# A two-layer attention and state-space kernel on one core: a new order for its opening

## The chip, the cores and the metric

The kernel runs on one core of one Trainium2 chip. A core has a tensor engine (PE; PEld is its weight load), a vector engine (DVE), a scalar engine (ACT), GpSimd (POOL) and a sync engine (SP) that here issues nearly all DMAs. Every engine works through its own instruction list in order and waits on semaphores. The metric is device time in microseconds (us): 1477.1 us, the median of three runs (1476.56 to 1478.08).

## The reference

Two layers work on one sequence of 512 tokens with 1024 features, in float32. What matters here is the way into the first layer:

```
h = rms_norm(x, norm_g[i])
(c_q, c_kv, k_rope, gate_a, z, xbc, ...) = split(h @ w_in[i])
o_a = mla(c_q, c_kv, k_rope, cos, sin) * silu(gate_a)     # rotated by cos, sin of the positions
o_b = ssd(z, xbc, dt_raw)                                 # state-space branch
o_c = sparse_attention(..., rel_bias[bucket(pos_q - pos_k)]) * silu(gate_c)
x = x + (g_a*(o_a @ w_br_a) + g_b*(o_b @ w_br_b) + g_c*(o_c @ w_br_c)) @ w_out[i]
x = x + sigmoid(x @ w_ple_gate[i]) * (p[i] @ w_ple[i])
```

Three things in it do not need `h`: `p @ w_ple`, the bias table `rel_bias[bucket(...)]`, and the cosines and sines of the positions. They can be worked out before the first layer's tiles.

## The kernel before

Activations lie as [feature, token]: a tile is 128 features by 512 tokens. A float32 product is made of three: activations and weights are each split into a high and a low part (ACT copies the high part, DVE subtracts it to get the low part), and `mm` multiplies high by high (L235), low weights by high (L236) and high by low (L243). `wload` issues one weight load of 512 KB on SP (L223), the copy on ACT (L224) and the subtraction on DVE (L225).

The order of PE is that of the Python code (`manual_schedule` for PE). DVE, ACT, POOL and SP get their lists from a scheduler by priority, so the place of an instruction there is not that of its line. All lists are fixed when the program is built.

The opening of layer 0 works like this:

- `setup` loads two tiles of p and their first weights. `rel_setup` loads positions and the bias's 32 rows with SP (L326 to L334), and makes thresholds and steps of the bias on POOL and DVE (L335 to L359).
- `run` loads the eight tiles of x on SP (L1313); `stat_add` squares each on ACT (L405) and adds it up on DVE (L406).
- `ple` makes p @ w_ple, four tiles of six products for each of two weight units. PE has these products to fill its time.
- `rel_bias` makes the distance bias in 32 blocks; a block is four mask tiles (DVE L376, some on ACT L374), 12 narrow products on PE (L388), an eviction (L392) and a store. The numbers in `EARLY` say how many blocks PE gets at four places of the opening: six in all. PRE, POST and PLE0 say how many pieces of `ple` come before, among and behind the sums of x's norm.
- `stat_sum` sums the squares on PE (L415), and a chain of 12 small DVE instructions (L424 to L430) makes 1 / rms. `stat_rows` spreads it over the partitions (PE L437). `normed` makes h: DVE multiplies (L448), ACT copies the high part (L449), DVE subtracts (L453), eight tiles.
- `rope_tables` makes the cosine and sine tables: one small load, 17 small DVE instructions, two sines on ACT with a table load, four stores to DRAM, two loads back, behind `normed`.
- `prep` starts the layer: the helper `three` multiplies three tiles of weights with all of h (L682, L683, L686: 72 products). Then come the c_q tiles, a second norm (L415 to L437 again), and the rotation of the keys (`rope`, L641 to L644), which needs the tables.

PSUM tiles of tag "mm" have three buffers; the high and low weights have three buffers each and the raw ones two.

Of the kernel before, what the change touches and what calls it, by code (L numbers as in the profile page):

```python
"""Two layers of MLA + SSD + sparse attention with a gated merge, activations kept [feature, token]."""
# [36 lines left out]
# smallest distance that falls into each of the 32 distance buckets  # L38
# [3 lines left out]
# ---------------------------------------------------------------- columns of w_in, in the order used here  # L42
# [13 lines left out]
# units of weights: 128 partitions of up to 1024 numbers  # L56
# [13 lines left out]
for _i in range(4):  # L70
    # followed by the keys of the two heads, from w_ukv
    _unit(("uq", _i), "uq", [96 * _h + _d for _h in (2 * _i, 2 * _i + 1) for _d in range(64)])
# [15 lines left out]
# ---------------------------------------------------------------- layout of the per-feature vectors  # L88
# [8 lines left out]
def pack(i):  # L97
    """Inputs laid out for the kernel; nothing is computed."""
    o = {}
# [41 lines left out]
    # numbers that depend on shapes alone  # L141
# [11 lines left out]
    for k in range(5):  # L153
        c[:, 408 + k] = 4.0 * (r >= 128 - 32 * k)  # the last k groups of 32 rows
# [4 lines left out]
class Build:  # L159
# [19 lines left out]
    # ---- SBUF in slots of 2 KB per partition  # L179
# [28 lines left out]
    # ---- weights: load, split into two parts of 12 bits each whose sum is exact  # L208
# [19 lines left out]
    def mm(self, ps, w, off, acts, t=slice(0, T)):  # L228
        """ps[128 features, tokens] += W^T act over the k tiles of acts, float32 from parts"""
# [23 lines left out]
    # ---- constants and tables  # L253
    def setup(self):
# [7 lines left out]
        self.prefetch(0, ("ple", 0))  # L262
        self.rel_setup()
# [18 lines left out]
    def rope_tables(self):  # L282
        """cosines, and sines with their signs, 32 rows four times over; worked out as [16 frequencies x 8, 64 tokens]"""
# [16 lines left out]
        # the rounding of k may leave r a little outside of [-pi, pi]  # L300
# [17 lines left out]
    def rel_setup(self):  # L318
        """positions from the first one on, thresholds, and the steps of the distance bias from bucket to bucket"""
        nc, I, cc = self.nc, self.I, self.c  # L320
        nc.sync.dma_start(cc[:, 384:416], I["c"][:, 384:416])
        # one row per bucket and query of four
# [3 lines left out]
        nc.sync.dma_start(d[:, 0], bass.AP(tensor=rb.tensor, offset=rb.offset, ap=[[8, 32], [0, 4], [1, 8]]))  # L326
        nc.sync.dma_start(d[4:128, 1], bass.AP(tensor=rb.tensor, offset=rb.offset, ap=[[8, 31], [0, 4], [1, 8]]))
        self.posi = self.slot(I32)
        nc.sync.dma_start(self.posi, bass.AP(tensor=I["pos"].tensor, offset=I["pos"].offset, ap=[[0, 128], [1, T]]))
        p0 = self.posi[:, 0:1]  # L330
        pq = self.slot(I32, (128, 128))
        nc.sync.dma_start(pq, I["posq"])
        last = self.const.tile([128, 1], F32, name="rbl")
        nc.sync.dma_start(last, bass.AP(tensor=rb.tensor, offset=rb.offset + 8 * 31, ap=[[0, 16], [1, 8], [1, 1]]))  # L334
# [4 lines left out]
        # masks of 0 and 1 take the steps, masks of -1 and 1 take half of them, and half of their sum is added  # L339
# [21 lines left out]
    def rel_bias(self):  # L361
        """8 * rel_bias[bucket(pos_q - pos_k)] into DRAM as [head, query, key], by sums over the buckets'
        thresholds: 32 buckets of 4 queries are the 128 rows of a product."""
# [35 lines left out]
    # ---- root mean square over the features, for each token, on every partition (PSUM)  # L399
# [9 lines left out]
    def stat_sum(self, s, dim, cs=range(4), fill=None):  # L409
        """1 / rms, [token, block of 128 tokens]"""  # L410
# [29 lines left out]
    def normed(self, xs, g, R):  # L440
        """parts of x * g * R"""
# [19 lines left out]
    # ---- pieces of work are generators, which yield what they put on the tensor engine in units of 512 columns  # L461
# [13 lines left out]
    @staticmethod  # L475
    def mix(*gens):
        """in turns"""
        gens = list(gens)
        while gens:
            for g in list(gens):  # L480
                try:
                    yield next(g)
                except StopIteration:
                    gens.remove(g)

    def weave(self, main, n, *tracks):
        """n pieces of main with other work, lists of (generator, cost), each spread evenly over them"""
# [14 lines left out]
    # ---- one tile of h @ w_in  # L502
# [9 lines left out]
    def gate2(self, ps):  # L512
        """2 silu"""
# [6 lines left out]
    # ---- p @ w_ple / 2 into DRAM  # L520
# [24 lines left out]
    # ---- softmax of one block of 128 queries; its transpose goes to PT  # L545
# [11 lines left out]
    def turned(self, u, qt, PT):  # L557
        """parts of the transpose of one block of 128 queries, [keys, queries]"""
# [21 lines left out]
    def attention(self, logits, V, PT, done):  # L580
        """logits(h, qt): probabilities of one block of queries; V(h, kb): [128 keys, high | low].
        Three stages, each a block of queries behind the one before; two pieces per block."""
# [31 lines left out]
    def gated(self, o, g):  # L614
        """parts of o * (g / 2)"""
# [6 lines left out]
    # ---- tiles that several branches need  # L622
    def common(self, ps):
# [7 lines left out]
        # four sets of keys, two heads of which are in use; the rotated part is common to all heads  # L631
# [5 lines left out]
    def rope(self, t, hi, lo, r=slice(0, 128)):  # L637
        """parts of the rotated rows"""
# [9 lines left out]
    def mla_rope(self, l, i):  # L648
        """the rotated part of four heads' queries"""
# [19 lines left out]
    # ---- MLA  # L669
    def prep(self, l, more):  # L670
        """what the attention needs, the chains of one norm under the products of the next tiles"""
        nc = self.nc

        def three(names):
            """tiles side by side, as the parts of h arrive"""
# [67 lines left out]
    def mla_pair(self, l, j):  # L743
        """keys and queries of heads 2j and 2j + 1"""
# [53 lines left out]
    # ---- sparse attention  # L798
    def stacked(self, l, name, j, out):
        """two heads of 64: [high; low] of the first, [low; high] of the second"""  # L800
# [9 lines left out]
    def dsa_keys(self, l, ps):  # L810
# [9 lines left out]
        # values: [high | low] for each block of keys  # L820
# [5 lines left out]
    def index(self, l, j):  # L826
        """scores of two index heads, for the queries from 128 on"""
# [25 lines left out]
    def topk(self):  # L853
        """the 128 largest of each row, the first of equals first"""
# [45 lines left out]
    # ---- SSD  # L900
    def ssd_steps(self, l):
        """dt, its sums within the chunks, and the decays, [token, chunk and head]"""
# [15 lines left out]
        # log(1 + e) = 2 atanh(e / (2 + e))  # L918
# [38 lines left out]
    def conv(self, l, t):  # L957
        """silu of the causal convolution"""
# [12 lines left out]
    def ssd(self, l, g):  # L971
        """one of two groups of eight heads"""
# [7 lines left out]
        def sums(i):  # L980
            """the sums of the steps of two heads, the same in all partitions"""
# [37 lines left out]
        def decays(i):  # L1019
            """C B^T exp(sum of the steps between), one tile for each of two heads, and the decays from the start"""  # L1020
# [4 lines left out]
            for e in range(2):  # L1025
# [3 lines left out]
                # above the diagonal the mask in cb decides, and exp stays finite  # L1029
# [62 lines left out]
    def gate_y(self, k):  # L1092
        """y silu(z) and its square, when both are there"""
# [20 lines left out]
    # ---- sigmoid(merge) * (o @ w_br), times two, summed over the branches  # L1114
# [6 lines left out]
    def branch(self, l, name, u, o, gates, done):  # L1121
        """one unit of weights of o @ w_br"""
# [11 lines left out]
    def layer(self, l, xs, s):  # L1134
# [20 lines left out]
        if l == 0:  # L1155
            self.rope_tables()
            # halves of the convolution's weights: silu(2u) = u (1 + tanh u)
# [94 lines left out]
        # the last tiles in two halves of the tokens, so that the output of one overlaps the products of the other  # L1252
# [28 lines left out]
    def last(self, x, k, t, R):  # L1281
        """two tiles of the result"""
# [9 lines left out]
    def pgate(self, l, m, x1, x1p, w=None, t=slice(0, T)):  # L1292
        """x += 2 sigmoid(x @ w_ple_gate) * p @ w_ple / 2"""
# [11 lines left out]
    def run(self):  # L1305
        nc = self.nc
        with self.tc.manual_schedule(engines={mybir.EngineType.PE}):
            self.setup()
            self.rb = self.rel_bias()
            xs, s = [], self.slot()  # L1310
            for k in range(8):
                x = self.slot()
                nc.sync.dma_start(x, self.I["x"][k])  # L1313
                xs.append(x)
                self.stat_add(s, x, k == 0)
# [16 lines left out]
PLE0 = 4  # L1332
# [34 lines left out]
```

## Time and profile before

| | |
|---|---|
| median of three runs | 1477.1 us |
| span of the profiled execution, first to last instruction | 1478.6 us |
| PE busy | 1433.6 us (97%) |
| DVE busy | 1110.5 us (75%) |
| ACT busy | 719.6 us (49%) |
| POOL busy | 135.5 us (9%) |

The profiled execution's own time is told only as its span, 1.5 us above the median of the runs. PE is the engine that is busy nearly always. The 40 slices of the page, 37 us each, show PE at six tenths in the first and the last slice, at eight in the second, and full in the others. The change is in the first two slices.

### The profile page before, as it was taken

Reading aid. Unit: us, or ns where it says so; the run is one execution under the profiler, and the core shown is the slowest. Engines: PE = TensorE matmul, PEld = TensorE weight load, DVE = VectorE, ACT = ScalarE, POOL = GpSimd, SP = SyncE. Lnnn points to the kernel's source line nnn. Section 1 sums busy time; section 2 is a strip of 40 time slices with the busy share of each in tenths; the row PEclk is TensorE's granted clock in tenths of the full one; section 3 lists DMA queues with packets and bytes.
Section 4 is the critical chain, followed back from the end, with each engine's and each line's share of the span. In section 5 each row is a group of like instructions: output and inputs, shape, how many; then the busy total and the mean of one; then the engine's idle time right before and its main releaser. Section 6 shows DMA issues by size and latency. Waiting matters only on the chain.

```text
span 1478.6 us, 20229 instructions
## 1 busy us (share of the span) xinstructions
PE 1433.6 (97%) x7244; PEld 1154.1 (78%) x7244; DVE 1110.5 (75%) x2346; ACT 719.6 (49%) x1367; POOL 135.5 (9%) x129
## 2 busy tenths in 40 slices
PE   6899999999999999999999999999999999999996
PEld 4777877777887777888878788888788777788886
DVE  7668776997888987654475697889888898775446
ACT  7447778524665342432344476632465644342332
POOL 0000000012220221000001000000322123100000
PEclk9999999999999999999999999999999999999998
DMA  7433222443333322443353322232333333234331
GB/s 260 135 94 102 83 88 79 125 126 96 102 100 122 114 93 72 157 148 98 124 171 99 111 74 74 90 99 90 115 107 102 105 114 108 72 124 146 115 98 59
DMA packets 67610, 162.40 MB, mean 110 GB/s; under 512 B 9237, under 2 KB 21653, under 8 KB 67509
## 3 DMA queue, kind: packets, MB, share of 16 engines
q1 hardware_dynamic: 67509, 161.11, 34.8%
q8 instruction: 57, 0.93, 0.3%
q14 instruction: 44, 0.36, 0.1%
HBM read 142.27 MB, written 13.83 MB: 106 GB/s over the span
## 4 chain that ended last, share of the span: by engine, by line
PE 80%; DVE 12%; DMA 3%; ACT 3%; issue 2%; POOL 1%; SPq 0%; DVEq 0%; ACTq 0%; POOLq 0%
PE p L235 22%; PE p L243 21%; PE p L236 21%; PE p L601 3%; DVE wl L225 2%; PE p L562 2%; DVE s L1033 2%; DMA s<-cum_d 2%; DVE s L965 1%; ACT wh L224 1%; PE p L388 1%; DVE s L1036 1%; PE p L682 1%; PE p L780 1%; PE p L683 1%
## 5 line engine op out<-in xcount | busy, mean ns | idle before, releaser
L235 PE MATMUL p<-s,wh 128*128 128x512 f32 (+1 forms) x1644 | 657.3, 401 | 8.1 <-ACT wh L224 8.1
L236 PE MATMUL p<-s,wl 128*128 128x512 f32 (+1 forms) x1644 | 646.5, 394 | 1.2 <-DVE wl L225 1.2
L243 PE MATMUL p<-s,wh 128*128 128x512 f32 (+1 forms) x1644 | 432.8, 395 | 0.0
L224 ACT ACTIVATE wh<-wr 128x1024 fp32r<-128x1024 f32 (+2 forms) x214 | 223.6, 1045 | 351.6 <-PE p L243 236.2
L235 PEld LDWEIGHTS p<-s,wh 128*128 128x128 f32 x1644 | 311.3, 189 | 74.4 <-ACT wh L224 8.1
L236 PEld LDWEIGHTS p<-s,wl 128*128 128x128 f32 x1644 | 311.5, 190 | 69.2 <-DVE wl L225 2.6
L225 DVE TENSOR_TENSOR wl<-wr,wh 128x1024 fp32r<-128x1024 f32 (+2 forms) x214 | 264.1, 1234 | 119.0 <-ACT wh L224 118.1
L243 PEld LDWEIGHTS p<-s,wh 128*128 128x128 f32 x1644 | 300.4, 188 | 67.2 <-issue 2.8
L552 ACT ACTIVATE s<-s,m 128x128 f32<-128x128 f32 (+3 forms) x128 | 71.5, 558 | 66.9 <-DVE m L551 66.5
L571 ACT ACTIVATE s<-p 128x256 fp32r<-128x256 f32 (+1 forms) x192 | 65.7, 342 | 58.6 <-PE p L562 31.5
L572 DVE TENSOR_TENSOR s<-p,s 128x256 fp32r<-128x256 f32 (+1 forms) x192 | 71.6, 374 | 15.1 <-ACT s L571 13.7
L880 POOL TENSOR_TENSOR s<-s,s 128x256 f32<-128x256 f32 (+2 forms) x48 | 58.1, 1229 | 142.8 <-DMA s<-bias_d 75.2
L562 PE MATMUL p<-c,s 128*128 128x128 f32 x320 | 56.4, 274 | 5.6 <-DVE s L554 5.6
L562 PEld LDWEIGHTS p<-c,s 128*128 128x128 f32 x320 | 40.6, 140 | 23.6 <-issue 10.3
L1129 DVE SCALAR_TENSOR_TENSOR s<-s,p 128x512 f32<-128x512 f32 x48 | 32.5, 677 | 34.7 <-PE p L243 34.7
L405 ACT ACTIVATE s<-s 128x512 f32<-128x512 f32 (+1 forms) x44 | 26.2, 601 | 66.4 <-DVE s L1096 39.9
L554 DVE TENSOR_SCALAR s<-s,m 128x128 f32<-128x128 f32 (+3 forms) x128 | 52.4, 409 | 2.6
L965 DVE SCALAR_TENSOR_TENSOR s<-p,v,s 128x511 f32<-128x511 f32 (+2 forms) x72 | 53.2, 740 | 0.0
L863 DVE MATCH_REPLACE8 s<-m,s 128x256 f32<-128x256 f32 (+2 forms) x96 | 51.5, 541 | 0.0
L860 DVE MAX8 m<-s 128x8 f32<-128x256 f32 (+2 forms) x96 | 49.2, 547 | 0.0
L250 ACT ACTIVATE s<-s 128x512 fp32r<-128x512 f32 (+1 forms) x58 | 36.2, 625 | 26.1 <-DVE s L644 10.7
L251 DVE TENSOR_TENSOR s<-s,s 128x512 fp32r<-128x512 f32 (+1 forms) x58 | 43.2, 745 | 7.3 <-ACT s L250 6.9
(190 smaller groups left out, 1633.5 us busy)
## 6 DMA issues: line engine op xcount, KB each, us to landing
wr<-in_w_dram SPq DMA_DIRECT2D x204, 512.0 KB, 3.6
s<-cum_d SPq DMA_DIRECT2D x32, 256.0 KB, 3.6
s<-in_x_dram SPq DMA_DIRECT2D x16, 256.0 KB, 5.3
ple_d<-s SPq DMA_DIRECT2D x16, 256.0 KB, 3.8
s<-bias_d SPq DMA_DIRECT2D x16, 256.0 KB, 3.4
s<-ple_d SPq DMA_DIRECT2D x13, 256.0 KB, 2.7
s<-bias_d SPq DMA_DIRECT2D x16, 192.0 KB, 2.8
s<-s SPq DMA_DIRECT2D x44, 64.0 KB, 2.0
```

What stands on the lines that cost most here:

```text
L224: nc.scalar.activation(hi[:, :n], raw[:, :n], AF.Copy)
L225: nc.vector.tensor_sub(lo[:, :n], raw[:, :n], hi[:, :n].bitcast(F32))
L235: nc.tensor.matmul(ps[:, t], hi[:, c], ah[:, t], start=k == 0, stop=False)
L236: nc.tensor.matmul(ps[:, t], lo[:, c], ah[:, t], start=False, stop=False)
L243: nc.tensor.matmul(ps[:, t], hi[:, c], al[:, t], start=False, stop=k == n - 1)
L552: nc.scalar.activation(u[:, :n], u[:, :n], AF.Exp, bias=mx, scale=-1.0, accum_out=sm)
L554: nc.vector.tensor_scalar(u[:, :n], u[:, :n], rs, None, op0=OP.mult)
L562: nc.tensor.transpose(tp[:, 128 * kb:128 * kb + 128], u[:, 128 * kb:128 * kb + 128], self.ident)
L571: nc.scalar.activation(h_, src, AF.Copy)
L572: nc.vector.tensor_sub(l_, src, h_.bitcast(F32))
L880: nc.gpsimd.tensor_tensor(b[:, :n], b[:, :n], mask, OP.add)
L965: nc.vector.scalar_tensor_tensor(a[:, d:], ps[:, :T - d], w(3 - d), a[:, d:], op0=OP.mult, op1=OP.add)
```

## The change

It reorders the opening; from `prep` on no function is changed.

- `warm` (new) runs first: GpSimd fills one tile with ones, and PE gets 20 products of it whose result nobody reads.
- The x tiles are loaded in `setup`, directly behind the first weights of p, and no longer behind the position loads.
- The five loads of bias rows and positions are issued by GpSimd (`nc.gpsimd.dma_start`) and no longer by SP.
- x's squares and sums are emitted in front of the bias blocks; `rope_tables` is emitted behind `setup_rest`, ahead of the first weights of the layer, and no longer behind `normed`.
- PLE0 goes from 4 to 8 (all of the first unit of p @ w_ple before anything else), PRE for layer 0 from 2 to 0, EARLY from (2, 0, 2, 2) to (0, 0, 2, 4): no bias block ahead of the norm's sums, two behind them, four between `normed` and `prep`.

```diff
+    def warm(self):
+        nc = self.nc
+        a = self.slot(BF)
+        nc.gpsimd.memset(a[:], 1.0)
+        ps = self.ps("pv")
+        for i in range(WARM):
+            nc.tensor.matmul(ps[:], a[:, 0:128], a[:], start=True, stop=True)
+        self.rel(a)
...
-    def setup(self):
+    def setup(self, xs):
...
         self.ple_prep(0)
         self.prefetch(0, ("ple", 0))
+        for k, x in enumerate(xs):
+            nc.sync.dma_start(x, I["x"][k])
         self.rel_setup()
         self.prefetch(0, ("ple", 1))
...
-        nc.sync.dma_start(d[:, 0], bass.AP(tensor=rb.tensor, offset=rb.offset, ap=[[8, 32], [0, 4], [1, 8]]))
+        nc.gpsimd.dma_start(d[:, 0], bass.AP(tensor=rb.tensor, offset=rb.offset, ap=[[8, 32], [0, 4], [1, 8]]))
...
-        nc.sync.dma_start(self.posi, bass.AP(tensor=I["pos"].tensor, offset=I["pos"].offset, ap=[[0, 128], [1, T]]))
+        nc.gpsimd.dma_start(self.posi, bass.AP(tensor=I["pos"].tensor, offset=I["pos"].offset, ap=[[0, 128], [1, T]]))
...
         self.rel(*xs)
         if l == 0:
-            self.rope_tables()
...
-            self.setup()
-            self.rb = self.rel_bias()
-            xs, s = [], self.slot()
-            for k in range(8):
-                x = self.slot()
-                nc.sync.dma_start(x, self.I["x"][k])
-                xs.append(x)
+            self.warm()
+            xs, s = [self.slot() for _ in range(8)], self.slot()
+            self.setup(xs)
+            for k, x in enumerate(xs):
                 self.stat_add(s, x, k == 0)
+            self.rb = self.rel_bias()
             self.setup_rest()
+            self.rope_tables()
             for name in FIRST[:PF]:
                 self.prefetch(0, name)
...
-PLE0 = 4
-PRE = (2, 0)
+PLE0 = 8
+WARM = 20
+PRE = (0, 0)
-EARLY = (2, 0, 2, 2)
+EARLY = (0, 0, 2, 4)
```

Line numbers move: in the changed kernel the mask is L388, the bias product L400, the sum of squares L418, the norm's chain L436 to L442, its spread L449, h's multiplication L460, h's low part L465, the first products of `three` L694 and the weights' low part still L225.

PE's list between the spread norm and `three`. Names are output<-inputs: p are PSUM tiles, s are SBUF tiles, rbp the bias steps, wh and wl the weights. Each bias block is 12 products of one p tile, of which one row stands here. Before:

```order
L437 MATMUL p69_394<-c_74,m54_315 128x128 x4
...
L388 MATMUL p101_487<-s65_372,rbp0_113 32x512
...
L388 MATMUL p105_509<-s99_481,rbp0_113 32x512
...
L682 MATMUL p110_533<-s71_400,wh28_190 128x512
L683 MATMUL p110_533<-s71_400,wl28_191 128x512
```

The same place in the changed kernel:

```order
L449 MATMUL p65_392<-c_106,m48_307 128x128 x4
L235 MATMUL p91_450<-s13_111,wh22_176 128x512
...
L400 MATMUL p95_466<-s61_370,rbp0_153 32x512
...
L400 MATMUL p99_488<-s93_460,rbp0_153 32x512
...
L400 MATMUL p103_510<-s97_482,rbp0_153 32x512
...
L400 MATMUL p107_532<-s101_504,rbp0_153 32x512
...
L694 MATMUL p112_556<-s67_398,wh34_242 128x512
```

Four bias blocks and one tile of p now stand between the spread and `three`; before it was two blocks.

DVE's list around the making of h. s65, s66, s99, s100 before, and s93 to s102 after, are mask tiles of the blocks above; m are the norm's small numbers. Before:

```order
L376 TENSOR_SCALAR s65_372<-s10_121,thr_125 128x512 x2
...
L376 TENSOR_SCALAR s99_481<-s10_121,thr_125 128x512
L376 TENSOR_SCALAR s100_482<-s10_121,thr_125 128x512
...
L430 SCALAR_TENSOR_TENSOR m54_315<-m55_316,m54_315 128x4
L448 SCALAR_TENSOR_TENSOR s70_399<-s14_148,v_75,p69_394 128x512
...
L453 TENSOR_TENSOR s93_436<-s91_434,s92_435 128x512
L290 TENSOR_SCALAR s95_448<-s94_447,c_74 128x64
```

The same place in the changed kernel:

```order
L442 SCALAR_TENSOR_TENSOR m48_307<-m49_308,m48_307 128x4
...
L460 SCALAR_TENSOR_TENSOR s66_397<-s3_97,v_107,p65_392 128x512
L320 TENSOR_TENSOR s33_215<-s33_215 128x64
L322 TENSOR_SCALAR s34_216<-s32_214 128x64
L460 SCALAR_TENSOR_TENSOR s69_402<-s4_98,v_107,p65_392 128x512
...
L465 TENSOR_TENSOR s89_434<-s87_432,s88_433 128x512
L1171 TENSOR_SCALAR v_107<-v_107 128x60 x2
L388 TENSOR_SCALAR s93_460<-s21_161,thr_165 128x512 x2
L388 TENSOR_SCALAR s94_461<-s21_161,thr_165 128x512
...
L388 TENSOR_SCALAR s102_505<-s21_161,thr_165 128x512
```

Before, the masks of both blocks stand ahead of h's first multiplication and the table's arithmetic (L290) behind h's last subtraction. Now the masks of the last three blocks (nine instructions) stand behind h's last subtraction, and the table's arithmetic stands ahead of it.

The start of DVE's list, where wl is the low part of p's first weights. Before:

```order
L251 TENSOR_TENSOR s3_80<-s1_77,s2_79 128x512
L251 TENSOR_TENSOR s6_86<-s4_83,s5_85 128x512
L335 TENSOR_TENSOR rbd_96<-rbd_96 128x8
L225 TENSOR_TENSOR wl6_90<-wr6_91,wh6_89 128x1024
L338 TENSOR_SCALAR rbw_107<-rbd_96,c_74 128x8 x4
```

The same place in the changed kernel:

```order
L347 TENSOR_TENSOR rbd_136<-rbd_136 128x8
L251 TENSOR_TENSOR s14_112<-s12_109,s13_111 128x512
L251 TENSOR_TENSOR s17_118<-s15_115,s16_117 128x512
L225 TENSOR_TENSOR wl17_122<-wr17_123,wh17_121 128x1024
L418 TENSOR_TENSOR s11_105<-s11_105,s24_188 128x512
```

The instruction that waits for the bias rows (rbd), now loaded by GpSimd, is DVE's first.

## Rows read from the trace of the kernel before

**Rows 1.** Windows: stage, its us; busy PE, PEld, DVE, ACT, POOL; clock; DMA; GB/s.

```profile
8.00:33.38 25.38, 22.49 (x133) 14.39 (x133) 23.15 (x67) 20.16 (x36) 1.39 (x2) 0.93 0.86 284
33.38:51.00 17.62, 17.26 (x72) 13.49 (x73) 14.01 (x32) 10.14 (x17) 0.00 (x0) 1.00 0.45 155
```

**Rows 2.** Waits of PE, first 115 us: waiter <- releaser: us, times, longest.

```profile
PE p L437 <- DVE m L430: 5.0, 2, 4.8
PE p L682 <- ACT s L449: 0.7, 2, 0.4
```

**Rows 3.** Timeline of PE: start, us, engine, line, op, tiles [idle before <- releaser].

```profile
33.38 0.50 PE L682 MATMUL p<-s,wh 128*128 128x512 f32 x1 [0.35 <-ACT s L449]
...
51.02 0.40 PE L235 MATMUL p<-s,wh 128*128 128x512 f32 x1
...
58.68 0.28 PE L415 MATMUL p<-c,s 128*128 128x1 f32 x2
...
63.10 0.60 PE L664 MATMUL p<-c,s 128*128 128x128 f32 x4
...
68.53 0.84 PE L437 MATMUL p<-c,m 128*128 128x128 f32 x4 [4.83 <-DVE m L430]
```

**Rows 4.** Timeline of DVE where the rotation waits for its table.

```profile
64.10 0.68 DVE L643 TENSOR_TENSOR s<-s,sin 32x512 f32<-32x512 f32 x1 [4.89 <-DMA sin<-rope_d]
```

**Rows 5.** Windows of PE alone behind that wait: busy, granted clock, DMA, GB/s.

```profile
68.00:69.00 1.00, 0.47 (x4) 0.89 0.27 66
69.00:70.00 1.00, 1.00 (x4) 0.50 0.35 86
...
72.00:73.00 1.00, 1.00 (x5) 0.90 0.80 172
```

**Rows 6.** Timeline of DVE up to the making of h.

```profile
8.06 1.23 DVE L225 TENSOR_TENSOR wl<-wr,wh 128x1024 fp32r<-128x1024 f32 x1
9.21 0.63 DVE L338 TENSOR_SCALAR rbw<-rbd,c 128x8 f32<-128x8 f32 x4
...
10.90 0.60 DVE L351 CAST s<-s 128x512 f32<-128x512 int32 x1 [1.07 <-POOL s L348]
...
13.17 2.06 DVE L376 TENSOR_SCALAR s<-s,thr 128x512 bf16<-128x512 f32 x5
...
16.32 0.68 DVE L406 TENSOR_TENSOR s<-s,s 128x512 f32<-128x512 f32 x1
16.92 0.48 DVE L376 TENSOR_SCALAR s<-s,thr 128x512 bf16<-128x512 f32 x1
...
26.49 0.16 DVE L424 TENSOR_SCALAR m<-p 128x4 f32<-128x4 f32 x1 [0.16 <-PE p L415]
26.57 1.23 DVE L225 TENSOR_TENSOR wl<-wr,wh 128x1024 fp32r<-128x1024 f32 x1
```

**Rows 7.** The same, from the chain's end through h's eight tiles.

```profile
30.56 0.16 DVE L429 SCALAR_TENSOR_TENSOR m<-m,m 128x4 f32<-128x4 f32 x1
30.75 0.16 DVE L430 SCALAR_TENSOR_TENSOR m<-m,m 128x4 f32<-128x4 f32 x1
...
33.46 4.69 DVE L448 SCALAR_TENSOR_TENSOR s<-s,v,p 128x512 f32<-128x512 f32 x7
...
38.07 4.90 DVE L453 TENSOR_TENSOR s<-s,s 128x512 fp32r<-128x512 f32 x8
```

**Rows 8.** Timeline of ACT: first weights, and a later table load.

```profile
6.97 1.06 ACT L224 ACTIVATE wh<-wr 128x1024 fp32r<-128x1024 f32 x1 [2.39 <-DMA wr<-in_w_dram]
...
101.65 1.28 ACT L515 ACT_TABLE_LOAD   x1
102.94 0.60 ACT L515 ACTIVATE s<-p 128x512 f32<-128x512 f32 x1
```

**Rows 9.** DMA issue of the position rows, and their reader on POOL.

```profile
4.19 2.64 SPq L329 DMA_DIRECT2D s<-in_pos_dram  x1
...
9.83 1.04 POOL L348 TENSOR_TENSOR s<-s 128x512 int32<-128x512 int32 x1 [9.00 <-DMA s<-in_pos_dram]
```

More of the change, by code (lines that the diff above doesn't have):

```diff
@@ L325, in rel_setup @@
         nc.gpsimd.memset(d[:, 1], 0.0)
-        nc.sync.dma_start(d[:, 0], bass.AP(tensor=rb.tensor, offset=rb.offset, ap=[[8, 32], [0, 4], [1, 8]]))
-        nc.sync.dma_start(d[4:128, 1], bass.AP(tensor=rb.tensor, offset=rb.offset, ap=[[8, 31], [0, 4], [1, 8]]))
+        nc.gpsimd.dma_start(d[:, 0], bass.AP(tensor=rb.tensor, offset=rb.offset, ap=[[8, 32], [0, 4], [1, 8]]))
+        nc.gpsimd.dma_start(d[4:128, 1], bass.AP(tensor=rb.tensor, offset=rb.offset, ap=[[8, 31], [0, 4], [1, 8]]))
         self.posi = self.slot(I32)
-        nc.sync.dma_start(self.posi, bass.AP(tensor=I["pos"].tensor, offset=I["pos"].offset, ap=[[0, 128], [1, T]]))
+        nc.gpsimd.dma_start(self.posi, bass.AP(tensor=I["pos"].tensor, offset=I["pos"].offset, ap=[[0, 128], [1, T]]))
         p0 = self.posi[:, 0:1]
         pq = self.slot(I32, (128, 128))
-        nc.sync.dma_start(pq, I["posq"])
+        nc.gpsimd.dma_start(pq, I["posq"])
         last = self.const.tile([128, 1], F32, name="rbl")
-        nc.sync.dma_start(last, bass.AP(tensor=rb.tensor, offset=rb.offset + 8 * 31, ap=[[0, 16], [1, 8], [1, 1]]))
+        nc.gpsimd.dma_start(last, bass.AP(tensor=rb.tensor, offset=rb.offset + 8 * 31, ap=[[0, 16], [1, 8], [1, 1]]))
         nc.vector.tensor_sub(d[:, 2], d[:, 0], d[:, 1])
@@ L1307, in run @@
         with self.tc.manual_schedule(engines={mybir.EngineType.PE}):
-            self.setup()
-            self.rb = self.rel_bias()
-            xs, s = [], self.slot()
-            for k in range(8):
-                x = self.slot()
-                nc.sync.dma_start(x, self.I["x"][k])
-                xs.append(x)
-                self.stat_add(s, x, k == 0)
+            self.warm()
+            xs, s = [self.slot() for _ in range(8)], self.slot()
+            self.setup(xs)
+            for k, x in enumerate(xs):
+                self.stat_add(s, x, k == 0)
+            self.rb = self.rel_bias()
             self.setup_rest()
+            self.rope_tables()
             for name in FIRST[:PF]:
```

## The prediction

> **What bounds the kernel now.** I read the stages first, then PE's waits, then the two timelines around them. PE is full from the first products of `three` on: from 33.38 to 51.00 it is busy 17.26 of 17.62 us [rows 1], and the next tile starts at 51.02 [rows 3]. So a microsecond by which `three` starts earlier or later, or by which PE waits behind it, is one of the kernel's time; the stretch ahead of 33.38 counts only by when it ends. Behind `three` one wait is large: PE stands still 4.83 us before the second spread norm at 68.53 [rows 2, 3], which waits for a chain on DVE, which has the rotation's product with the sine ahead of it, and that waited 4.89 us for the sine table to come from DRAM, until 64.10 [rows 4]. After the wait the granted clock is 0.50, the lower level of 1.2 GHz, for a little over three microseconds, and 1.00 again in the course of the window from 72 [rows 5].
>
> So the change can win the rope wait and its clock, and win or lose by the start of `three`.
>
> **What goes: the rope wait.** The tables are now worked out ahead of h and not behind it, and are loaded before the keys are rotated. Then the second norm's 12 small instructions follow their sums at once. At 0.195 us each (30.56 to 30.75 [rows 7]) they take 2.4 us, while PE still has products from the last sum at 58.68 to 63.70 [rows 3], 5 us. So nothing is late in its place and 4.83 us go. The clock's loss goes too: 0.11 + 3 x 0.50 + 0.10 = 1.71 us, as the three windows from 69 to 72 read alike [rows 5]. Together 6.54.
>
> **What moves: DVE's list up to `three`.** In the built order nine masks of the last three bias blocks stand behind h's last subtraction, and PE has these blocks ahead of `three`. PE works in order, so `three` cannot begin before DVE is through all of h and nine masks, though the first tile of h is there long before. Before, the masks were done ahead of h. I add up DVE's list by steps from one start to the next.
>
> Start: the low part of p's first weights began at 8.06 [rows 6], behind ACT's copy at 6.97 [rows 8]. Their load keeps its place, fourth on SP, but behind an x tile of 256 KB and no longer a piece of 16 KB. At the 284 GB/s of the opening [rows 1] that is at most 0.9 us; I take half, 8.6.
>
> Up to the sums: this split 1.15 (8.06 to 9.21), seven additions of squares at 0.60 (16.32 to 16.92) 4.2, the bias setup 0.63 + 2.27 (10.90 to 13.17) = 2.9 [rows 6], and 0.4 of waits for squares, which on ACT now alternate with the evictions of p @ w_ple (between 0 and 1; an estimate). That is 17.25. The second split waits for its copy, 0.5, and takes 1.15: 18.9. Behind it five products and three sums remain on PE, 1.5 us at 0.235 and 0.11: 20.4.
>
> The chain: 12 small steps with seven of the rope's, four masks and two splits between. A small one costs 0.08 beside other work (26.49 to 26.57 [rows 6]) and 0.195 alone; I take 0.10, since here they are mixed: 1.9. The masks cost 0.41 (2.06 for five [rows 6]): 1.64; the splits 2.3. So it ends at 26.2, against 30.91 before [rows 7]: 4.7 earlier.
>
> From there to `three`: two small 0.2, two masks 0.82, h's first multiplication 0.66, a wait for the sine 0.8 (ACT has two masks and the table load of 1.28 [rows 8] in front), three small 0.3, seven multiplications 4.61 (33.46 to 38.07), a split 1.15, eight subtractions 4.90 [rows 7], two small 0.2, nine masks 3.69; together 17.3: 43.5. The last block's 12 narrow products, four side by side, add some three steps of 0.235: 44.2. In the kernel before the same stretch was 2.5 us (30.91 to 33.38).
>
> `three` itself took 17.64 (33.38 to 51.02), with 0.7 of waits for h [rows 2, 3]; with h complete 16.9, a product each 0.235. It ends at 61.1, not 51.02: 10.1 later. The three blocks in front of it follow some 13 us of idle PE, so the clock begins low, as in rows 5. Its loss is between 0 (the blocks' products take the time) and 1.7; I take 0.7.
>
> **Sum.** 10.1 + 0.7 - 6.54 = +4.3 us. It is made against the profiled execution's own span of 1478.6, which stands 1.5 above the median; as a difference it goes onto the median: 1481.4 us.
>
> **At nothing.** The 20 products of `warm`, at two steps of 0.235 each some 9.4 us, run while PE has no weights (8.03 before); if they end a microsecond late, the first unit's 24 products still end before the sums. Fewer loads on SP save issue time (2.64 for the positions alone [rows 9]) that shows only in the start taken above. From 62 us on all products are the same; the later weights have more lead, and PE waits there hardly at all.
>
> The table load is followed at once by the next activation (101.65 + 1.28, then 102.94), so I price a switch at 1.28 [rows 8]. The Trainium skill (ScalarE: Activation LUTs, What ACT_TABLE_LOAD costs) states a drain of about 1.38 us more for each switch. By the page the wait for the sine grows by that, and the estimate would be 1482.8; no drain shows in the row, so I leave it out.
>
> **Bounds.** Without any wait on DVE, from 8.06 on, the list alone takes 33.2 us: 1.15 + 4.2 + 2.9 + 1.15, then three masks and two small (1.4), the chain 5.8 and 16.5. `three` at 41.9, the clock unhurt: +1.3; small steps at 0.08 take another 0.5. That gives 1477.9. On the other side stand the lower clock's full 1.7 (1.0 more than taken), the 28 small steps at 0.195 (2.7 more) and the late loads of the first rival (2.2).
>
> **Rivals.**
> *GpSimd's loads are late.* DVE's first instruction now waits for two loads of bias rows from GpSimd's queue, with p's split behind it. No row shows a DMA from that queue. The nearest are SP's: 2.64 us of issue and 5.64 from issue to POOL's start (4.19 to 9.83 [rows 9]). At 2.64 an issue from about 1 us on, the second row load is issued by 6.3 and, 3.0 later as there, landed by 9.3; the two splits of p take 1.3 and a step of 0.2 more, and the list starts at 10.8 and not 8.6. That is 2.2 late and makes 1483.6. If issues there are short, it costs nothing; I take nothing, since the row loads are of 4 KB. The Trainium skill (SBUF — State Buffer, SBUF: two separate sides) says that a DMA from GpSimd has its descriptors written by GpSimd itself, which certain DVE instructions lock out. By that rule the loads could only be late while DVE works, and DVE has little to do there; it supports the rival weakly.
> *The list runs without waits.* The bounds above: `three` between 41.3 and 42.8, a time of 1477.9 to 1480. For it speaks that DVE was busy 23.15 of 25.38 us [rows 1], hardly waiting; against it that ACT and PE have to deliver four times on the way. No change that can be measured.
> *Faster: the norm sets the start.* If the masks did not hold PE, `three` would begin 2.5 us behind the chain, at 28.7, 4.7 earlier, and with the rope wait the time would be 1465.9. It decides from a start of `three` before 37. Against it stands the order, and 33.2 us of DVE work that would have to fit into 28.
>
> **How the numbers follow.** 0.2% is 3 us, about what a measurement of this kernel tells from no change. Forecast 0.54, GpSimd late 0.12, both slower: 0.66. Without waits, within 0.2%: 0.22. Faster: 0.12, for the third rival and for a price of mine that is far off. The likeliest case alone spans 1480 to 1484; the range for 8 in 10 goes from 1477.5, the second rival's end, to 1487, where all three of the other bounds come together.
>
> **What would show it.** In the changed kernel's profile PE should be idle some 13 us between the first and the second of the four bias blocks behind the spread norm, waiting for DVE's masks (L388); its first L694 near 44; h's last subtraction (L465) near 39.5; the spread norm (L449) near 26; no wait before the second L449, and no low clock there. DVE's first instruction should end its wait before 7. The forecast is wrong if L694 starts before 41 or after 48, if the masks come earlier than I say, or if a wait behind `three` takes the place of the rope's.

## The result, and the profile after

The changed kernel takes 1492.99 us (median of four runs, 1491.79 to 1495.47), the kernel before 1476.83 in the same runs: a ratio of 1.0109, 95% interval 1.0095 to 1.0124, or 16.2 us more. The forecast was 1481.4 and a range up to 1487. Slower was right, the size was not: the time lies outside the range, and the forecast's own sign of being wrong, a first L694 after 48, came (54.76). The profiled execution spans 1493.7 us, 15.1 more than the one of before.

PE's waits in the first 130 us (waiter <- releaser: us, times, longest):

```profile
PE p L400 <- DVE s L388: 12.9, 1, 12.9
PE p L236 <- DVE wl L225: 5.3, 3, 4.2
...
PE p L449 <- DVE m L442: 0.2, 1, 0.2
```

The first row is the wait that the forecast described: bias products on PE that wait for masks on DVE. The last stands where [rows 2] had 5.0: the rope wait is gone. PE's timeline (start, us, engine, line, op, tiles, and in brackets the idle time before and its releaser):

```profile
9.80 0.49 PE L235 MATMUL p<-s,wh 128*128 128x512 f32 x1 [2.45 <-ACT wh L224]
14.50 0.80 PE L236 MATMUL p<-s,wl 128*128 128x512 f32 x1 [4.20 <-DVE wl L225]
...
25.86 0.63 PE L236 MATMUL p<-s,wl 128*128 128x512 f32 x1
26.29 0.42 PE L427 MATMUL p<-c,s 128*128 128x1 f32 x2
26.57 1.20 PE L243 MATMUL p<-s,wh 128*128 128x512 f32 x2
27.57 0.42 PE L427 MATMUL p<-c,s 128*128 128x1 f32 x2
...
34.33 0.65 PE L449 MATMUL p<-c,m 128*128 128x128 f32 x4 [0.24 <-DVE m L442]
...
50.02 4.81 PE L400 MATMUL p<-s,rbp 128*32 128x512 bf16 x36 [12.87 <-DVE s L388]
54.76 0.80 PE L694 MATMUL p<-s,wh 128*128 128x512 f32 x1
...
72.06 0.40 PE L235 MATMUL p<-s,wh 128*128 128x512 f32 x1
...
84.57 0.60 PE L449 MATMUL p<-c,m 128*128 128x128 f32 x4
```

Against [rows 3]: `three` starts at 54.76 and not at 33.38, it ends at 72.06 and not at 51.02, and the second spread norm (84.57) follows without a wait. From the end of `three` to the first product of the values (L742, at 96.2; before L730, at 81.8) it is 24.2 us and not 30.7. So 21.0 us are lost up to the end of `three`, 6.6 are won behind it, and 0.7 in all that follows make the 15.1. The granted clock (last but two) is at its lower level, 0.50 or 1.2 GHz, where bias products follow the idle time and where the sums of the norm are made:

```profile
25.00:30.00 5.00, 5.00 (x16) 4.22 (x15) 3.03 (x16) 2.94 (x5) 0.00 (x0) 0.50 0.80 268
50.00:55.00 5.00, 4.98 (x37) 1.92 (x38) 3.92 (x10) 1.51 (x3) 0.00 (x0) 0.50 0.34 107
```

DVE's timeline, answering to [rows 6, 7]:

```profile
11.07 0.17 DVE L347 TENSOR_TENSOR rbd<-rbd 128x8 f32<-128x8 f32 x1 [11.07 <-DMA rbd<-in_rb_dram]
11.17 1.29 DVE L251 TENSOR_TENSOR s<-s,s 128x512 fp32r<-128x512 f32 x2
12.38 2.06 DVE L225 TENSOR_TENSOR wl<-wr,wh 128x1024 fp32r<-128x1024 f32 x1
14.37 3.27 DVE L418 TENSOR_TENSOR s<-s,s 128x512 f32<-128x512 f32 x4
...
23.37 1.23 DVE L225 TENSOR_TENSOR wl<-wr,wh 128x1024 fp32r<-128x1024 f32 x1 [0.67 <-ACT wh L224]
24.52 0.48 DVE L388 TENSOR_SCALAR s<-s,thr 128x512 bf16<-128x512 f32 x1
...
28.02 0.16 DVE L436 TENSOR_SCALAR m<-p 128x4 f32<-128x4 f32 x1 [1.97 <-PE p L427]
...
34.12 0.15 DVE L442 SCALAR_TENSOR_TENSOR m<-m,m 128x4 f32<-128x4 f32 x1
...
38.07 0.22 DVE L320 TENSOR_TENSOR s<-s 128x64 f32<-128x64 f32 x1 [2.11 <-ACT s L318]
...
44.47 4.90 DVE L465 TENSOR_TENSOR s<-s,s 128x512 fp32r<-128x512 f32 x8
...
49.48 4.43 DVE L388 TENSOR_SCALAR s<-s,thr 128x512 bf16<-128x512 f32 x11
```

It begins 3.8 us later than forecast, waits for the bias rows until 11.07, and is later still at each station. GpSimd had issued those rows long before, and works on the positions just when DVE splits:

```profile
1.33 0.71 POOL L338 DMA_DIRECT2D rbd<-in_rb_dram  x1
2.03 1.53 POOL L339 DMA_DIRECT2D rbd<-in_rb_dram  x1
...
12.05 1.32 POOL L360 TENSOR_TENSOR s<-s 128x512 int32<-128x512 int32 x1 [6.83 <-DMA s<-in_pos_dram]
```

### The profile page after: what moved, and what is told of

It reads as the page before. It is cut to its first block, busy times and chain, and to the rows that moved or that the text cites. A ratio compares the mean times of both kernels' runs of the same rounds, so it can differ in the third digit from the quotient of the medians.

```text
span 1493.7 us, 20270 instructions
## 1 busy us (share of the span) xinstructions
PE 1440.3 (96%) x7264; PEld 1155.7 (77%) x7264; DVE 1110.7 (74%) x2346; ACT 721.3 (48%) x1367; POOL 140.7 (9%) x135
## 4 chain that ended last, share of the span: by engine, by line
PE 74%; DVE 17%; ACT 3%; issue 2%; DMA 2%; POOL 1%; DVEq 0%; ACTq 0%; POOLq 0%
PE p L243 20%; PE p L236 20%; PE p L235 20%; DVE wl L225 3%; PE p L613 3%; PE p L574 2%; DVE s L875 2%; DVE s L1045 2%; DMA s<-cum_d 2%; DVE m L872 1%; DVE s L977 1%; ACT wh L224 1%; PE p L400 1%; PE p L694 1%; DVE s L1048 1%
## 5 line engine op out<-in xcount | busy, mean ns | idle before, releaser
L225 DVE TENSOR_TENSOR wl<-wr,wh 128x1024 fp32r<-128x1024 f32 (+2 forms) x214 | 266.4, 1245 | 131.3 <-ACT wh L224 130.0
L584 DVE TENSOR_TENSOR s<-p,s 128x256 fp32r<-128x256 f32 (+1 forms) x192 | 71.6, 374 | 14.7 <-ACT s L583 13.5
L574 PEld LDWEIGHTS p<-c,s 128*128 128x128 f32 x320 | 40.6, 140 | 24.4 <-issue 10.5
L1045 DVE TENSOR_SCALAR s<-s,m 128x128 f32<-128x128 f32 x128 | 38.4, 349 | 13.1 <-DMA s<-cum_d 6.8
L892 POOL TENSOR_TENSOR s<-s,c 128x128 f32<-128x128 f32 x16 | 10.3, 645 | 374.9 <-PE p L243 176.2
```

The lines of the kernel that those rows point to most:

```text
L225: nc.vector.tensor_sub(lo[:, :n], raw[:, :n], hi[:, :n].bitcast(F32))
L574: nc.tensor.transpose(tp[:, 128 * kb:128 * kb + 128], u[:, 128 * kb:128 * kb + 128], self.ident)
L584: nc.vector.tensor_sub(l_, src, h_.bitcast(F32))
L1045: nc.vector.tensor_scalar(d[:, k], d[:, k], self.cum[:, 16 * c + h:16 * c + h + 1], 0.0, op0=OP.subtract, op1=OP.min)
```

## The experiments

Each ratio is to the kernel before on the same chip (1476.8 beside the changed kernel, 1477.7 to 1478.1 beside the others). "To values" is the time from the first product of `three` to the first product of the values; with it one sees whether the rope wait is there.

| kernel | us | against before, 95% | `three` starts | to values |
|---|---|---|---|---|
| before | 1476.8 | | 33.4 | 48.4 |
| changed | 1493.0 | 1.0095 to 1.0124 | 54.8 | 41.4 |
| e1 before, tables moved up | 1476.3 | 0.9977 to 0.9996 | 36.3 | 42.0 |
| e2 changed, old order on PE | 1479.5 | 0.9999 to 1.0018 | 41.5 | 41.0 |
| e3 changed, rows by ACT | 1493.5 | 1.0080 to 1.0115 | 54.2 | 41.1 |
| e4 e2 and e3 | 1480.6 | 0.9999 to 1.0020 | 42.7 | 41.1 |
| e5 changed, rows by SP ahead of x | 1486.9 | 1.0047 to 1.0077 | 48.5 | 41.0 |
| e6 changed, masks ahead | 1485.3 | 1.0039 to 1.0074 | 47.4 | 41.1 |
| e7 e2 without the constant products | 1479.2 | 1.0004 to 1.0023 | 40.6 | 41.0 |
| e8 e1, tables on GpSimd | 1480.4 | 1.0007 to 1.0025 | 41.7 | 41.2 |
| e9 e5 and e6 | 1484.1 | 1.0028 to 1.0055 | 44.0 | 41.2 |
| e10 e2 and e5 | 1477.3 | 0.9986 to 1.0003 | 38.6 | 41.3 |
| e11 before, tables among h's subtractions | 1478.6 | 1.0000 to 1.0017 | 33.5 | 48.9 |
| e12 e1, squares added by GpSimd | 1480.6 | 1.0011 to 1.0028 | 43.5 | 41.1 |
| e13 e3, rows as 30 and 1 | 1491.0 | 1.0064 to 1.0095 | 51.0 | 41.1 |
| e14 e11, tables loaded in quarters | 1472.1 | 0.9946 to 0.9971 | 33.5 | 42.0 |
| e15 before, tables loaded in quarters | 1472.9 | 0.9948 to 0.9974 | 33.1 | 42.3 |

The start of `three` and the rope wait carry the column of times. Without the rope wait, the time less the start of `three` lies between 1437 and 1440 in fifteen kernels; with it (before, e11) it is 1443.4 and 1445.1. So, to within 3 us, the opening costs what it delays `three`.

**The order on PE and its masks (e2, e6, e7).** e2 takes back the three numbers of the order:

```diff
-PLE0 = 8
+PLE0 = 4
-PRE = (0, 0)
+PRE = (2, 0)
-EARLY = (0, 0, 2, 4)
+EARLY = (2, 0, 2, 2)
```

> The changed kernel with PE's order of before (EARLY, PLE0 and PRE as they were), all else as changed: the masks of the last blocks then stand on DVE ahead of the chain of the norm and not behind h. Theory A (the masks behind h hold PE for 12.9 us): the first product of three starts near 41 and not at 54.8, and the time is 1476 to 1481. Theory B (the late start of DVE's list costs most, the order little, since DVE has the same work ahead of three either way): three starts near 50, 1488 or more.

It took 13.5 us off, as theory A said, though the chain of the norm came later than in the changed kernel (its spread at 38.77 and not 34.33), since the masks now stand ahead of it and among its steps. The spread norm (L449), the two blocks behind it and `three` follow each other:

```profile
38.77 0.65 PE L449 MATMUL p<-c,m 128*128 128x128 f32 x4
39.35 1.48 PE L400 MATMUL p<-s,rbp 128*32 128x512 bf16 x24
41.50 0.50 PE L694 MATMUL p<-s,wh 128*128 128x512 f32 x1 [0.66 <-ACT s L461]
```

e6 leaves PE's order alone and makes masks of up to four blocks ahead:

```diff
-        nxt = masks(31)
+        made, nxt = 32, deque()
         for blk in reversed(range(32)):
-            n, k, tiles = nxt
-            if blk:
-                nxt = masks(blk - 1)
+            while made > max(0, min(blk - 1, max(25, blk - DEEP))):
+                made -= 1
+                nxt.append(masks(made))
+            n, k, tiles = nxt.popleft()
```

> The changed kernel, PE's order untouched, with the masks of the last blocks made earlier in DVE's list: six of them stand behind h's multiplications and ahead of h's eight subtractions, which before them took 4.9 us. Theory A (PE waits for the masks, wherever they stand): the first product of three starts 4.5 to 6.5 us earlier, at 48 to 50, with some waits of three for h's low parts, and the time is 1486.5 to 1489.5. Theory B (what counts is the blocks' place in PE's order, or h): no gain, 1491.5 or more.

Theory A again, and more than the 4.5 to 6.5 us expected: 7.3 us on the start of `three`, 7.7 on the time. In its DVE timeline nine masks, and not six, stand ahead of the subtractions, and PE's blocks start behind them:

```profile
42.97 3.65 DVE L388 TENSOR_SCALAR s<-s,thr 128x512 bf16<-128x512 f32 x9
46.53 4.89 DVE L466 TENSOR_TENSOR s<-s,s 128x512 fp32r<-128x512 f32 x8
```

```profile
43.50 3.99 PE L401 MATMUL p<-s,rbp 128*32 128x512 bf16 x36 [7.14 <-DVE s L388]
47.42 0.50 PE L695 MATMUL p<-s,wh 128*128 128x512 f32 x1
```

e7 is e2 with the call of `warm` taken out (`-self.warm()`).

> The changed kernel with PE's order of before, as run earlier (1479.5), and without the 20 products on a constant at the start. Theory A (they run while PE has no weights and the clock is low again before the products that matter): the same time within 1.5 us. Theory B (they keep the clock up for the products of p): 2 to 4 us slower, and the granted clock of the first products of p is lower than with them.

The time stayed (1479.2 and 1479.5). With this order on PE the constant products neither help nor cost; with the order of the changed kernel no run leaves them out.

**The late rows (e3, e4, e5, e13).** e3 has ACT issue the two row loads (`nc.gpsimd.dma_start(d[...` becomes `nc.scalar.dma_start(d[...`), e4 does so in e2.

> The changed kernel with the two loads of bias rows issued by ACT instead of GpSimd; the positions stay on GpSimd's queue. Theory A (the late row loads cost what they delay at the head of DVE's list): DVE's first instruction starts by 8, p's first split by 9.5 and not at 12.4, and the time is 2.5 to 4 us less than the changed kernel's, 1489 to 1490.5. Theory B (DVE would wait for p, the positions or squares anyway): the time stays within 1.5 us of 1493.

> The changed kernel with both of the other two edits: PE's order of before, and the two loads of bias rows issued by ACT. If the two costs add up, the time is 1473 to 1477, as much below the run with the old order alone as the loads bring alone. If DVE's list has slack at the start once the masks no longer hold PE, it is the same as with the old order alone, within 1.5 us.

Both brought nothing, and the expectation of theory A failed at its first step: DVE still started late, though ACT had issued the second load by 2.7.

```profile
12.12 0.17 DVE L347 TENSOR_TENSOR rbd<-rbd 128x8 f32<-128x8 f32 x1 [12.12 <-DMA rbd<-in_rb_dram]
```

So GpSimd's queue alone doesn't make them late, and what rows on time would be worth is not tested by either. e5 issues the same loads on SP, ahead of all of x:

```diff
+        nc.sync.dma_start(d[:, 0], bass.AP(tensor=rb.tensor, offset=rb.offset, ap=[[8, 32], [0, 4], [1, 8]]))
+        nc.sync.dma_start(d[4:128, 1], bass.AP(tensor=rb.tensor, offset=rb.offset, ap=[[8, 31], [0, 4], [1, 8]]))
         for k, x in enumerate(xs):
             nc.sync.dma_start(x, I["x"][k])
```

> The changed kernel with the two loads of bias rows issued by SP, ahead of all of x; the positions stay on GpSimd's queue. Theory A (the row loads are late because x's loads are in front of or beside them): DVE's first small instruction starts by 8.5, p's first split by 10.5 instead of 12.4, the first product of three by 53, and the time is 1490 to 1491.5. Theory B (the list's head is set by the weights, the squares and PE as much as by the rows): p's first split comes earlier, but the chain of the norm still starts near 28 and the time stays within 1 us of 1493.

It won more than expected, 6.1 us:

```profile
9.03 0.17 DVE L348 TENSOR_TENSOR rbd<-rbd 128x8 f32<-128x8 f32 x1 [1.68 <-DMA rbd<-in_rb_dram]
9.46 1.23 DVE L225 TENSOR_TENSOR wl<-wr,wh 128x1024 fp32r<-128x1024 f32 x1 [0.27 <-ACT wh L224]
...
15.38 2.28 DVE L419 TENSOR_TENSOR s<-s,s 128x512 f32<-128x512 f32 x3 [0.25 <-ACT s L418]
...
25.62 0.16 DVE L437 TENSOR_SCALAR m<-p 128x4 f32<-128x4 f32 x1 [2.22 <-PE p L428]
...
34.12 0.23 DVE L325 TENSOR_TENSOR s<-s 128x64 f32<-128x64 f32 x1
```

The split is 2.9 us earlier. It is also no longer slowed by GpSimd, whose positions landed at 7.4, but longer waits for squares take that back before the chain. The rest comes later in the list: the chain is 0.5 shorter, the sine's reader (L325) no longer waits 2.1, because the built list now has three of h's multiplications ahead of it and not one, and the last three blocks take 4.0 us on PE and not 4.8. So e5 changes more than the rows: the built lists differ too, and SP now issues p's first weights ahead of the first x tile. How much of the 6.1 us is the rows alone is not shown. e13 cuts the second load of e3 in two:

```diff
-        nc.scalar.dma_start(d[4:128, 1], bass.AP(..., ap=[[8, 31], [0, 4], [1, 8]]))
+        nc.scalar.dma_start(d[4:124, 1], bass.AP(..., ap=[[8, 30], [0, 4], [1, 8]]))
+        nc.scalar.dma_start(d[124:128, 1], bass.AP(..., ap=[[0, 4], [1, 8]]))
```

> The changed kernel with the row loads issued by ACT, as in the run that brought nothing (1493.5, DVE's first instruction at 12.1), and one more edit: the second load, of 31 rows, is cut into 30 rows and one. Theory A (a load of 31 rows is slow beside x's traffic by its shape, since 31 rows can't be shared out over the DMA engines): DVE's first instruction starts by 8, p's first split by 10.5, the first product of three 3 to 6 us earlier, and the time is 1486.5 to 1490. Theory B (any small load beside x's loads lands late): DVE's first instruction at 11 or later, and 1492 or more.

Neither theory: DVE's first instruction at 9.8, `three` 3.2 earlier, the time 2.5 less than e3, which the two intervals do not separate. The load of 30 rows still took 8.2 us to land. With the rows ahead of x (e5) `three` starts 2.5 us earlier still; what holds a 4 KB load for 8 us beside x stays open.

**Both, and the old order (e9, e10).** These put edits together that are shown above.

> The changed kernel with two of the edits that won time singly: the row loads by SP ahead of x (1486.9 alone) and the last blocks' masks ahead of h's subtractions (1485.3 alone). If the late rows and the masks are two costs on one list, they add up: 6.1 and 7.7 below 1493, that is 1478 to 1480.5, with three at 40 to 42. If one hides part of the other, 1482 or more.

> The changed kernel with PE's order of before and the row loads by SP ahead of x. If the earlier head of the list is worth here what DVE's first split shows (2.9 us), the time is 1475.5 to 1477.5, 2 to 3.5 below the run with the old order alone. If x, now behind the rows, delays the squares as much as the rows gain, it stays at 1479 to 1481.

e10 came out as forecast, at the upper edge, and is level with the kernel before. Its `three` still starts 5.3 us later than there, which the rope wait pays back; 2.9 us are what the moved tables cost alone in the kernel before (e1), the rest stays open. e9 did not come out: `three` at 44.0 and not 40 to 42. There PE's own blocks became the limit, behind 5.71 us of waiting and at a granted clock of 0.50 (39.66 to 44.00):

```profile
39.66 4.42 PE L402 MATMUL p<-s,rbp 128*32 128x512 bf16 x35 [5.71 <-DVE s L389]
44.00 0.59 PE L696 MATMUL p<-s,wh 128*128 128x512 f32 x1
```

**The tables (e1, e8, e11, e12, e14, e15).** e1 moves the call of `rope_tables` in the kernel before to behind `setup_rest` (on DVE these are 14 instructions, L290 to L310, and not 17), e8 also gives its small operations to GpSimd (`nc.vector` becomes `nc.gpsimd`, a step of three operands becomes two).

> The kernel before with one edit: the rope tables are worked out ahead of h, right behind the loads of the constants. If the rope wait and its low clock are worth the 6.5 us of the prediction, the time is 1470 to 1473: 6.5 won, and up to 2.4 lost on DVE, where the tables' 12 small operations now stand ahead of h. The second spread norm should follow without a wait. If another wait takes the rope's place, or the tables delay the chain of the norm by more than they bring, the time is within 3 us of 1477.

> The kernel before with the rope tables moved up, as in the run with the tables alone (1476.3), but their small operations worked out by GpSimd and not by DVE. Theory A (the tables' operations on DVE delay h, and with it three by 2.9 us there): three starts near 33.5 again, the rope wait stays gone, and the time is 1472 to 1474.5. Theory B (three is late there through ACT, the blocks or the loads): three near 36 and 1475.5 to 1477. GpSimd's operations could also slow those of DVE beside them; then it is over 1477.

e1 won the rope wait (42.0 to the values and not 48.4), but lost 2.9 in front of `three`, more than allowed for, and gained only 1.6 on the time. e8 lost more: ACT waited 3.7 us for GpSimd's arithmetic before the sine (at 29.16), with the copy of the next weights behind it, and DVE's split behind that. e12 gives the additions of squares to GpSimd.

> The kernel before with the rope tables moved up as in the run with the tables alone (1476.3), and the seven additions of x's squares done by GpSimd and not by DVE, from whose list they take 4.2 us. Theory A (DVE's list sets the start of three): three starts 3 to 5 us earlier than the 36.3 of that run, and the time is 1472 to 1474, below both kernels. Theory B (the sums wait for ACT's squares and PE, or GpSimd is slower on them than DVE): the chain of the norm starts no earlier than 26, three at 35 or later, 1475.5 or more.

Theory B, and worse. Masks on DVE that take 0.41 each alone now alternate with GpSimd's additions: the seven that start while GpSimd adds are 1.42 us apart, the four behind them, with GpSimd done at 25.69, 0.40 again. (DVE in two windows of its timeline, then POOL.)

```profile
15.94 10.04 DVE L376 TENSOR_SCALAR s<-s,thr 128x512 bf16<-128x512 f32 x7
25.90 1.66 DVE L376 TENSOR_SCALAR s<-s,thr 128x512 bf16<-128x512 f32 x4
```

```profile
15.22 10.47 POOL L1319 TENSOR_TENSOR s<-s,s 128x512 f32<-128x512 f32 x7 [4.68 <-ACT s L1318]
```

e11 puts the tables between h's multiplications and subtractions (`normed` calls them there); e14 and e15 cut the loads of the tables, in e11 and in the kernel before:

```diff
-        for i, t in enumerate((self.cos, self.sin)):
-            a = self.rope_d[i]
-            nc.sync.dma_start(t, bass.AP(..., ap=[[0, 4], [T, 32], [1, T]]))
+        for j in (2, 0, 1, 3):
+            for i, t in ((1, self.sin), (0, self.cos)):
+                a = self.rope_d[i]
+                nc.sync.dma_start(t[32 * j:32 * j + 32], bass.AP(..., ap=[[T, 32], [1, T]]))
```

> The kernel before with one edit: the rope tables' operations stand on DVE among h's subtractions, behind h's multiplications and ahead of where they were. If the rope wait can go without a later start of three, three starts at 33.4 as in the kernel before, its first use of the sine no longer waits, and the time is 1470 to 1472.5, below both kernels and below the run with the tables ahead of h (1476.3). If the sine is still late for its first use, or the subtractions now hold three, it is 1474 or more.

> The run with the tables' operations among h's subtractions (1478.6, where the sine table still took 10 us from its issue to its use), with each of the two table loads cut into four loads of 32 rows, the quarter that the keys need first. Theory A (the load, which reads the same 32 rows four times in one DMA, is slow by its shape): the quarter lands within 4 us of its issue, the first use of the sine doesn't wait, three still starts at 33.5, and the time is 1471 to 1473.5, below both kernels. Theory B (the load is late because of the weight loads around it on SP's queue): the wait stays over 3 us, 1476 or more.

> The kernel before with the table loads cut into four quarters each as its only edit; nothing is moved. Theory A (the shape of the load makes the sine late): the wait of 4.9 us for the sine falls below 2, the wait of PE for the second norm falls with it, and the time is 1471.5 to 1474.5. Theory B (the issue comes too late behind weights and stores): the wait stays over 3 us, 1475.5 or more.

e11 kept `three` at 33.5 but not its gain: the sine, issued at 52.5, was used at 62.73. In e14 the quarter that is needed was issued at 50.4 and used at 55.35; of these 7.4 us, 2.1 are the earlier issue, since the sine now goes first (e11, then e14):

```profile
62.73 0.68 DVE L645 TENSOR_TENSOR s<-s,sin 32x512 f32<-32x512 f32 x1 [4.92 <-DMA sin<-rope_d]
```

```profile
55.35 0.68 DVE L646 TENSOR_TENSOR s<-s,sin 32x512 f32<-32x512 f32 x1 [1.93 <-DMA sin<-rope_d]
```

Both runs with quarters are below both kernels, with times as theory A says in both; the quarter of e14 still took 4.9 us, and its reader waited 1.93. That the load's shape matters can also be seen in the kernel before. From 57 to 58 its two table loads (issued at 53.32 and 56.51) are all that moves, and the mean busy share of the 16 DMA engines (last but one) is 0.26, which is four engines' work:

```profile
57.00:58.00 1.00, 1.00 (x7) 1.00 0.26 98
```

In e15, where nothing else is edited, the sine is issued at 57.9 and used at 61.8, while in the kernel before it was issued at 56.5 and used at 64.10 [rows 4]; its reader also stands nine steps further down the built list, so the 5 us are not the load's alone.

## Why the prediction was right in direction and wrong in size

**Right.** Three of the four bias blocks, and `three` behind them, wait on PE for masks behind h: 12.9 us of idle PE where "some 13" was forecast. e6, which moves only masks, shows that it is the masks and not h. The rope term of 6.54 measured 6.6. `three` with h complete took 17.30, forecast 16.9.

**Wrong: the sum for DVE's list, 44.2, which came to 54.8.** By its own stations:

| step | forecast | changed | e5 |
|---|---|---|---|
| first split starts | 8.6 | 12.38 | 9.46 |
| to the second split's end | 10.3 | 12.1 | 12.4 |
| to the chain's start | 1.5 | 3.5 | 3.75 |
| the chain | 5.8 | 6.25 | 5.7 |
| from there to `three` | 18.0 | 20.5 | 17.1 |
| `three` starts | 44.2 | 54.8 | 48.5 |

(The second split ends 1.15 behind its start.) Four terms fail.

*The start, 8.6, with the first rival.* "GpSimd's loads are late" happened; it had 0.12, and in the sum I took nothing: "If issues there are short, it costs nothing", and "the row loads are of 4 KB". The issues were short (0.71 and 1.53, over by 3.6), and DVE waited for the rows until 11.07 even so: the landing was late and not the issue. The rival's price was too small also: 2.2 on the start, which moved by 3.8. It left out what the delay pushes together: GpSimd's subtraction now runs beside DVE's split (2.06 and not 1.23). The Trainium skill's rule that I cited (SBUF — State Buffer, SBUF: two separate sides), on descriptors which GpSimd can't write while DVE works, did not act here: GpSimd's issues end by 5.2, with DVE idle until 11.07, and e3 is as late from ACT.

*The additions, "seven additions of squares at 0.60", and their waits, 0.4.* The 0.60 was read where a mask stands between two additions (16.32 to 16.92 [rows 6]). Directly behind one another, each on the sum of the one before, they are 0.80 apart: three take 2.28 in e5, with GpSimd idle, and four take 3.27 in the changed kernel, the first beside GpSimd. The wait for squares is near forecast in the changed kernel, 0.54, since DVE comes late. In e5, without the late rows, DVE stands 0.81, 1.18 and 0.25 for squares, 2.2 in all, mostly because x's tiles still arrive. I had priced ACT's turns with the evictions, and not the arrival of x.

*The sums, 1.5 "at 0.235 and 0.11".* PE had idled, and worked at the lower clock (0.50 from 25 to 30): the products stand about 0.43 apart (25.86 to 26.29), a sum's pair 0.28.

*The last stretch, 18.0.* I had counted a loss of clock in the last blocks, but too small: 36 products took 4.81 at 0.50, some 1.6 a block and not 0.7. The sine's wait was 2.1 and not 0.8. The table load itself was as priced from [rows 8], 1.28 and the sine at once behind it (36.49 to 37.78).

With the rows on time, as in e5, my sum would still have been 4.3 us short on `three` (48.5 against 44.2), and e5's time, 1486.9, would have been inside the range only at its end. Each station was taken as if the next engine ran at its full clock and its data had landed. The bounds added up small steps (28 of them, where the sum has 26), the clock and a rival of 2.2; none was for a list that waits for its inputs.

## What to carry to other kernels

Work out a moved opening as a chain that passes between engines: at each handover ask whether PE has been idle (behind 12.87 us of waiting its granted clock was 0.50 here) and whether the data has landed, and put such waits into the bounds. Before reordering to hide a late load, look at the load: cutting the two broadcast loads into quarters won 5 us here, while the reorder that hid the same wait lost 21 in front of it. Work that PE has ahead of its main stream must not depend on what another engine does last.

## What the runs showed of the hardware that was not expected

DVE and GpSimd can hold each other up by whole instructions: in e12 seven masks and seven additions alternate, 1.42 us apart, where a mask alone takes 0.40. Moving 4.2 us of additions off DVE cost `three` 7.2 (e12 against e1). The Trainium skill (SBUF — State Buffer, Who interferes with whom) says that the two share one pair of ports, which certain DVE instructions and GpSimd's hold for a whole instruction while the other waits; the trace agrees.

A load that reads the same 32 rows four times in one DMA needed 7.6 to 10.2 us from issue to use (before, e11), a quarter of it some 4 to 5 (e14, e15). The Trainium skill (DMA: Bandwidth & Descriptors, Why a DMA increments its semaphore by 16 and not by 1) says that a DMA runs on the largest number of engines, at most 16, that divides the outermost dimension of both sides, which is 4 for that load. The trace agrees: while only such loads move, the 16 engines are busy for 0.26, four of them. The row loads fit less well: by that rule 30 rows would run on 15 engines, and those of e13 still took 8.2 us.

The twenty constant products, from 1.3 to 7.3 us, did not keep PE's pace up for the products of p. Behind waits of 2.45 and 4.20 us those stood 0.43 apart, at a granted clock of 0.50 (15 to 17); e2, with them, has the same spacing, and so has e7 without, where the record of the clock reads 1.00 (13 to 17) and so doesn't account for it. In e5, where the waits were 1.07 and 0.76, the products stood 0.23 apart; no run leaves the constant products out there.
